# A hybrid layer in one core: two readers of a PSUM bank in a planned order, and the delta rule's state ahead of its output

## The chip, the core and the metric

The kernel runs on one core of a Trainium2 chip. A core has five engines with queues of their own: PE (TensorE, matmuls; PEld is its weight loads), DVE (VectorE, element by element), ACT (ScalarE, functions and copies), POOL (GpSimd) and SP (which issues DMAs here). Each engine takes its instructions in program order and waits on semaphores for the others. PE writes its products into PSUM, eight banks of 512 floats on each of 128 partitions, which ACT and DVE read; everything else lies in SBUF. The metric is the time of one execution on the device in microseconds, lower is better.

## The reference

Two blocks work one after the other on 512 tokens of width 2048. The first projects the tokens, runs a gated delta rule over 24 heads beside an attention over 256 memory rows, and projects back; the second runs an mLSTM and an HGRN2 mixer. The change lies in the delta rule, of which this is the core (chunks `n` of a head, in the kernel 4 chunks of 128 tokens, and the 24 heads in 12 pairs):

```python
def step(state, inp):
    u0_c, w_c, qk_c, qd_c, kd_c, cd_c = inp
    u = u0_c - jnp.einsum("bhcd,bhde->bhce", w_c, state)
    o = jnp.einsum("bhcd,bhde->bhce", qd_c, state) + jnp.einsum("bhcj,bhje->bhce", qk_c, u)
    state = cd_c[..., None, None] * state + jnp.einsum("bhcd,bhce->bhde", kd_c, u)
    return state, o
```

Here `u0` and `w` come from a triangular system of each chunk, solved by an explicit inverse.

## The kernel before

All tensors are float32. A projection multiplies weights and tokens that are each split into a high and a low part, so one step of 128 contracted columns (a k-step below) is three matmuls of 128x512 into one bank named `acc`. Weights arrive in pieces of four k-steps: SP loads `raw`, ACT rounds it to `hi`, DVE subtracts to get `lo`. At most three accumulators are open at once in this stage, and one gives its bank back when its evacuation has read it.

Around the projections run the small tasks. For each pair of heads `inverse` builds the inverse `XT` (`pp`, `px`, two products `p`; on DVE a transpose `Nb` and 31 rounds of a multiply and a reduction on `Xb`), and `rec_task` is the recurrence over the four chunks. One step of it is: `ks` (keys times state, PE), `rp` (two instructions on DVE), `up` (XT times rp, PE, one bank), then two readers of that bank, the copy `u` (ACT), which only the output needs, and the scaled `ud` (DVE), which the next state needs; then `pst` (PE) and the new state `S` (ACT in the first chunk, DVE after), and `o<-e,u` and `o<-gR,S` (PE), the two parts of the output. A recurrence starts only when the one before is done.

What sets the order is a planner that runs when the program is built. `Driver` keeps a clock for each engine, charges every instruction a cost (`act`, `tt`, `stt`, `ts`, `cp` and `mm`), and holds in `tau` when the value at hand will be ready. `run` takes the task of the best priority whose `tau` is not beyond PE's clock, else the next k-step of the projections, else it moves PE's clock on. The program that comes out is fixed: on each engine the instructions stand in that order, and semaphores are the only thing that moves at run time. A semaphore also keeps ACT and DVE from reading one PSUM bank at the same time: the one that is issued second waits for the first.

Two limits of the planner: tiles of 128x512 floats come from 75 slots, and `y_loader`, which fetches for the last gate projections what they multiply, takes a slot only while 24 others stay free, as long as the last recurrence isn't done. And the evacuations of those projections (`evac_z`) wait for that tile, with their accumulators still held.

Of the kernel before, what the change touches and what calls it, by code (L numbers as in the profile page):

```python
# [12 lines left out]
AF = mybir.ActivationFunctionType  # L13
ALU = mybir.AluOpType
AX = mybir.AxisListType
PSUM = bass.MemoryType.PSUM
# [5 lines left out]
NCH = T // C  # L22
# [10 lines left out]
def bc(ap, axis, n):  # L33

    a = ap.unsqueeze(axis)
    return a.broadcast_to(tuple(a.shape[:axis]) + (n,) + tuple(a.shape[axis + 1:]))


def v4(ap):
    return ap.rearrange("p (n c) -> p n c", n=NCH)  # L40


def free_size(ap):
    n = 1
    for s in ap.shape[1:]:
        n *= s
    return n


class Fut:  # L50

    def __init__(self):
        self.done, self.val, self.tau = False, None, 0.0
# [25 lines left out]
class Driver:  # L79
# [5 lines left out]
    def __init__(self, tc, wp, psp, sp):  # L85
        self.tc, self.nc, self.wp, self.psp, self.sp = tc, tc.nc, wp, psp, sp
        self.clk = dict(pe=0.0, act=0.0, dve=0.0, pool=0.0, sp=1.2)
        self.dq = 0.0
        self.tau = 0.0
        self.tasks = []  # L90
        self.units = []
        self.pieces = []
        self.i_unit = self.i_dma = self.i_hi = self.i_spl = self.i_mm = 0
        self.spl_end = []
        self.nbank, self.nacc, self.maxacc = 0, 0, 6
        self.bank_t = [0.0] * 8
        self.bank_of = {}
        self.live = 0
        self._dep, self._last = 0.0, None
        self.held = {}  # L100
        self.nslot = 0
        self.table = None
        self.nhead, self.head = 0, None


    def _on(self, e, cost, lat):
# [2 lines left out]
        self.tau = self.clk[e] + lat  # L109
        self._dep, self._last = dep, (e, self.tau)  # L110

    def act(self, out, in_, func, table=None, **kw):
        t = table or {AF.Exp: 1, AF.Ln: 1, AF.Silu: 2, AF.Sigmoid: 3}.get(func)
        cost = 0.11 + free_size(out) / 1200
        if t and t != self.table:
            self.table = t
            cost += 1.3
            if t == 1:
                self.nc.scalar.add_instruction(mybir.InstLoadActFuncSet(  # L119
                    name=self.nc.get_next_instruction_name(), act_func_set_id=EXP_LN))  # L120
        self.nc.scalar.activation(out=out, in_=in_, func=func, **kw)  # L121
        self._on("act", cost, LV)

    def _v(self, eng, n):
        if eng is None:
            self._on("dve", 0.08 + n / 960, LV)
            return self.nc.vector
        self._on("pool", 0.1 + n / 400, LV)
        return eng

    def tt(self, out, a, b, op, eng=None):
        self._v(eng, free_size(out)).tensor_tensor(out=out, in0=a, in1=b, op=op)  # L132

    def stt(self, out, a, s, b, op0, op1):
        self._v(None, free_size(out)).scalar_tensor_tensor(out=out, in0=a, scalar=s, in1=b, op0=op0, op1=op1)  # L135

    def ts(self, out, a, s1, op0, s2=None, op1=None, eng=None):
        kw = dict(op1=op1) if op1 is not None else {}
        self._v(eng, free_size(out)).tensor_scalar(out=out, in0=a, scalar1=s1, scalar2=s2, op0=op0, **kw)

    def cp(self, out, a, eng=None):
        self._v(eng, free_size(out)).tensor_copy(out=out, in_=a)

    def set(self, out, v, eng=None):
        self._v(eng, free_size(out)).memset(out, v)
# [12 lines left out]
    def mm(self, out, lhsT, rhs, start=True, stop=True, tr=False):  # L158
        n = free_size(out)
        if lhsT.dtype == F32R:  # L160
            c = max(0.107, n / 2400)
        elif tr:
            c = 0.105
        else:
            c = max(0.055 if lhsT.shape[0] <= 32 else 0.107 if lhsT.shape[0] <= 64 else 0.2, n / 600)
            if lhsT.shape[0] <= 64:
                c = min(c, 0.107)
        self.nc.tensor.matmul(out, lhsT=lhsT, rhs=rhs, start=start, stop=stop,  # L168
                              is_transpose=True if tr else None)
        self._on("pe", c, LP)  # L170
# [28 lines left out]
    def free(self, *tiles):  # L199
        self.live -= len(tiles)  # L200
        for t in tiles:
            del self.held[t.tensor.name]

    def small(self, shape, tag, bufs=2):
        return self.sp.tile(list(shape), F32, tag=tag, bufs=bufs, name=tag)

    def bank(self, name="pw"):
        while True:
            if self.nbank >= 8:
                yield lambda: self.nbank < 8  # L210
                continue
            t = self.bank_t[0]
            if max(t, self.tau) <= self.clk["pe"]:
                break
            self.tau = max(t, self.tau)
            yield
        return self.bank_now(name)
# [26 lines left out]
    def give(self, fut, val=True):  # L244
        fut.done, fut.val, fut.tau = True, val, self.tau

    def need(self, fut):
        while not fut.done:
            yield fut
        self.tau = max(self.tau, fut.tau)  # L250
        return fut.val
# [153 lines left out]
def build(ctx: ExitStack, tc: tile.TileContext, A, out):  # L405
# [17 lines left out]
    d = Driver(tc, wp, psp, sp)  # L423
    d.nslot = NSLOT
    act, tt, stt, ts, cp, mm = d.act, d.tt, d.stt, d.ts, d.cp, d.mm
# [33 lines left out]
    n = 0  # L459
# [27 lines left out]
    def split(src, hi, lo):  # L487
        act(hi, src, AF.Copy)
        tt(lo, src, hi, SUB)
# [553 lines left out]
    def rec_task(g):  # L1043
        if g:
            yield from need(f_r[g - 1])
        kT, XT = yield from need(f_k[g])
        qds, e2s, cd, Kt, q2 = yield from need(f_q[g])
        vb0 = yield from need(f_v[2 * g])
        vb1 = yield from need(f_v[2 * g + 1])
        vbs = [vb0, vb1]  # L1050
        o0 = yield from bank("o")
        o1 = yield from bank("o")
        os_ = [o0, o1]
        S = None
        for n in range(NCH):
            s = slice(n * C, (n + 1) * C)
            if n:
                yield
                ks = yield from bank("ks")
                mm(ks[:, :256], kT[:, s], S.rearrange("p h c -> p (h c)"))  # L1060
                t0 = d.tau
                for hh in range(2):
                    mm(os_[hh][:, s], S[:, hh], qds[hh][:, s], start=True, stop=False)
                d.tau = t0
                rp = small([128, 2, C], "rp")
                for hh in range(2):
                    stt(rp[:, hh], ks[:, hh * C:(hh + 1) * C],
                        gate["nbeg"][:, n, 2 * g + hh:2 * g + hh + 1], vbs[hh][:, n], MUL, ADD)
                d.free_bank()
                rr = [rp[:, 0], rp[:, 1]]  # L1070
            else:
                rr = [vbs[0][:, 0], vbs[1][:, 0]]
            yield
            up_ = yield from bank("up")
            up = up_[:, :256].rearrange("p (h c) -> p h c", h=2)
            for hh in range(2):
                mm(up[:, hh], XT[hh][:, n], rr[hh])
            u = small([128, 2, C], "u")
            t0 = d.tau
            act(u, up, AF.Copy)  # L1080
            tu = d.tau
            d.tau = t0
            if n < NCH - 1:
                ud = small([128, 2, C], "ud")
                tt(ud, up, bc(gate["kdec"][:, n, 2 * g:2 * g + 2], 2, C), MUL)
                d.free_bank()
                yield
                ps_ = yield from bank("pst")
                pst = ps_[:, :256].rearrange("p (h c) -> p h c", h=2)
                mm(pst, Kt[:, n], ud.rearrange("p h c -> p (h c)"))  # L1090
                Sn = small([128, 2, C], "S", 3)
                if n:
                    for hh in range(2):
                        stt(Sn[:, hh], S[:, hh], cd[:, hh, n:n + 1], pst[:, hh], MUL, ADD)
                else:
                    act(Sn, pst, AF.Copy)
                d.free_bank()
                S = Sn
                ts_ = d.tau
            else:  # L1100
                d.tau = max(d.tau, tu)
                d.free_bank()
            d.tau = tu
            yield
            for hh in range(2):
                mm(os_[hh][:, s], u[:, hh], e2s[hh][:, n], start=(n == 0), stop=True)
            if n < NCH - 1:
                d.tau = max(ts_, d.clk["pe"])
        free(kT, Kt, *XT, *qds, *e2s, *vbs)
        give(f_r[g])  # L1110
        left = [q2, q2]
        for hh in range(2):
            d.spawn(out_task(2 * g + hh, os_[hh], left), 11 + g)
# [925 lines left out]
```

## Time and profile before

| | |
|---|---|
| three runs | 2903.46, 2903.51 and 2904.26 us, median 2903.51 us |
| the profiled execution | 2903.78 us, of which the span of the trace is 2902.0 us |
| PE busy | 2857.8 us, 98% of the span |
| DVE busy | 1720.4 us, 59% |
| ACT busy | 1409.6 us, 49% |
| the 12 recurrences | from about 408 to 1265 us of the span |

The profile lists for each engine when it was busy, and for the idle time ahead of an instruction which other engine's instruction ended it. PE is the engine to watch: its weight loads overlap its matmuls, and whatever time it stands still is added to the end. A line number in a row is often that of a helper (L121 is every ACT instruction, L132 and L135 most of DVE's, L168 every matmul), so rows are told apart by the names of their tiles, output first. `hi`, `lo` and `acc` belong to the projections. The granted clock is 1.00 when TensorE runs at 2.4 GHz and 0.50 at 1.2 GHz.

### The profile page before, as it was taken

Reading aid. Unit: us, or ns where it says so; the run is one execution under the profiler, and the core shown is the slowest. Engines: PE = TensorE matmul, PEld = TensorE weight load, DVE = VectorE, ACT = ScalarE, POOL = GpSimd, SP = SyncE. Lnnn points to the kernel's source line nnn. Section 1 sums busy time; section 2 is a strip of 40 time slices with the busy share of each in tenths; the row PEclk is TensorE's granted clock in tenths of the full one; section 3 lists DMA queues with packets and bytes.
Section 4 is the critical chain, followed back from the end, with each engine's and each line's share of the span. In section 5 each row is a group of like instructions: output and inputs, shape, how many; then the busy total and the mean of one; then the engine's idle time right before and its main releaser. Section 6 shows DMA issues by size and latency. Waiting matters only on the chain. (4 is left out here: it accounts for less than half of the span.)

```text
span 2902.0 us, 41149 instructions
## 1 busy us (share of the span) xinstructions
PE 2857.8 (98%) x15032; PEld 2392.6 (82%) x15032; DVE 1720.4 (59%) x3287; ACT 1409.6 (49%) x2651; POOL 102.6 (4%) x198
## 2 busy tenths in 40 slices
PE   8999999999999999999999999999999999999998
PEld 7877888788888878888888888888888888888887
DVE  6745677777777767745333364556655655544446
ACT  7544645555555555544222334445555556433444
POOL 2000000000000000000000000000000000000001
PEclk9999999999999999999999999999999999999999
DMA  7423323232322322344433433222222222333224
GB/s 237 149 77 96 123 88 98 95 102 81 102 95 92 98 88 95 106 167 123 127 122 119 139 116 105 93 82 82 83 81 81 88 85 86 117 120 111 93 96 149
DMA packets 179020, 311.05 MB, mean 107 GB/s; under 512 B 25344, under 2 KB 32128, under 8 KB 178816
## 3 DMA queue, kind: packets, MB, share of 16 engines
q1 hardware_dynamic: 178816, 308.41, 33.2%
q8 instruction: 118, 1.93, 0.3%
q14 instruction: 86, 0.70, 0.1%
HBM read 292.34 MB, written 15.99 MB: 106 GB/s over the span
## 5 line engine op out<-in xcount | busy, mean ns | idle before, releaser
L132 DVE TENSOR_TENSOR lo<-raw,hi 128x512 fp32r<-128x512 f32 (+1 forms) x956 | 646.6, 689 | 606.5 <-ACT hi L121 583.0
L121 ACT ACTIVATE hi<-raw 128x512 fp32r<-128x512 f32 (+1 forms) x964 | 591.8, 621 | 846.1 <-PE acc L168 745.2
L168 PE MATMUL acc<-xh,hi 128*128 128x512 f32 x1424 | 583.1, 410 | 0.0
L168 PE MATMUL acc<-xl,hi 128*128 128x512 f32 x1424 | 555.7, 390 | 0.0
L168 PE MATMUL acc<-xh,lo 128*128 128x512 f32 x1408 | 551.1, 391 | 2.4 <-DVE lo L132 2.4
L168 PE MATMUL acc<-x2h,hi 128*128 128x512 f32 x1040 | 415.6, 400 | 0.0
L168 PE MATMUL acc<-x2l,hi 128*128 128x512 f32 x1040 | 405.2, 390 | 0.0
L168 PE MATMUL acc<-x2h,lo 128*128 128x512 f32 x1024 | 399.7, 390 | 0.0
L168 PEld LDWEIGHTS acc<-xh,lo 128*128 128x128 f32 x1408 | 264.4, 188 | 61.6 <-DVE lo L132 3.6
L168 PEld LDWEIGHTS acc<-xh,hi 128*128 128x128 f32 x1424 | 268.2, 188 | 52.2 <-issue 1.7
L168 PEld LDWEIGHTS acc<-xl,hi 128*128 128x128 f32 x1424 | 268.4, 189 | 50.4 <-issue 1.7
L168 PE MATMUL acc<-ph,hi 128*128 128x512 f32 x768 | 298.8, 389 | 0.0
L168 PE MATMUL acc<-pl,hi 128*128 128x512 f32 x768 | 298.8, 389 | 0.0
L168 PE MATMUL acc<-ph,lo 128*128 128x512 f32 x768 | 298.8, 389 | 0.0
L168 PEld LDWEIGHTS acc<-x2h,lo 128*128 128x128 f32 x1024 | 192.2, 188 | 41.4
L168 PEld LDWEIGHTS acc<-x2h,hi 128*128 128x128 f32 x1040 | 195.6, 188 | 37.2
L168 PEld LDWEIGHTS acc<-x2l,hi 128*128 128x128 f32 x1040 | 195.7, 188 | 37.0
L168 PEld LDWEIGHTS acc<-ph,lo 128*128 128x128 f32 x768 | 144.1, 188 | 30.0
L168 PEld LDWEIGHTS acc<-pl,hi 128*128 128x128 f32 x768 | 144.1, 188 | 30.0
L168 PEld LDWEIGHTS acc<-ph,hi 128*128 128x128 f32 x768 | 144.1, 188 | 29.8
L135 DVE SCALAR_TENSOR_TENSOR cv<-acc,c_dn_conv,cv 128x511 f32<-128x511 f32 x144 | 107.2, 747 | 21.3 <-ACT cv L121 17.8
L132 DVE TENSOR_TENSOR Xb<-Xb,Nb 128x16 f32<-128x16 f32 (+30 forms) x372 | 114.5, 308 | 8.7
(323 smaller groups left out, 3712.8 us busy)
## 6 DMA issues: line engine op xcount, KB each, us to landing
raw<-w_qkv SPq DMA_DIRECT2D x192, 256.0 KB, 3.2
raw<-w_out SPq DMA_DIRECT2D x192, 256.0 KB, 2.9
raw<-w_z SPq DMA_DIRECT2D x128, 256.0 KB, 3.1
raw<-w_pg SPq DMA_DIRECT2D x76, 256.0 KB, 3.2
gR<-dgc SPq DMA_DIRECT2D x48, 256.0 KB, 4.1
raw<-w_k SPq DMA_DIRECT2D x32, 256.0 KB, 5.4
raw<-w_v SPq DMA_DIRECT2D x32, 256.0 KB, 3.4
raw<-w_xq SPq DMA_DIRECT2D x32, 256.0 KB, 3.1
```

Source lines behind the costliest of these rows:

```text
L121: self.nc.scalar.activation(out=out, in_=in_, func=func, **kw)
L132: self._v(eng, free_size(out)).tensor_tensor(out=out, in0=a, in1=b, op=op)
L135: self._v(None, free_size(out)).scalar_tensor_tensor(out=out, in0=a, scalar=s, in1=b, op0=op0, op1=op1)
L168: self.nc.tensor.matmul(out, lhsT=lhsT, rhs=rhs, start=start, stop=stop, is_transpose=True if tr else None)
```

## The change

Two things change. In the step of the recurrence `ud` is issued ahead of `u`, so that DVE reads the bank first and ACT second; the planner's time for `u` then lies behind `ud`, and the bank counts as free only after `u`. And the planner notes who last read a PSUM bank: an instruction that reads a bank last read by another engine is timed behind it.

```diff
+def in_psum(ap):
+    return ap.tensor.space == "PSUM"
...
+    def _reads(self, e, *aps):
+        self._bank = [ap.tensor.name for ap in aps if in_psum(ap)]
+        for b in self._bank:
+            if b in self.reader and self.reader[b][0] != e:
+                self.tau = max(self.tau, self.reader[b][1])
+
+    def _read(self, e):
+        for b in self._bank:
+            self.reader[b] = (e, self.tau)
+
     def act(self, out, in_, func, table=None, **kw):
+        self._reads("act", in_)
...
         self._on("act", cost, LV)
+        self._read("act")
...
     def tt(self, out, a, b, op, eng=None):
+        self._reads("dve", a, b)
         self._v(eng, free_size(out)).tensor_tensor(out=out, in0=a, in1=b, op=op)
+        self._read("dve")
...
             u = small([128, 2, C], "u")
-            t0 = d.tau
-            act(u, up, AF.Copy)
-            tu = d.tau
-            d.tau = t0
             if n < NCH - 1:
                 ud = small([128, 2, C], "ud")
                 tt(ud, up, bc(gate["kdec"][:, n, 2 * g:2 * g + 2], 2, C), MUL)
-                d.free_bank()
+            td = d.tau
+            act(u, up, AF.Copy)
+            tu = d.tau
+            d.free_bank()
+            d.tau = td
+            if n < NCH - 1:
                 yield
...
                 ts_ = d.tau
-            else:
-                d.tau = max(d.tau, tu)
-                d.free_bank()
             d.tau = tu
```

`stt`, `ts` and `cp` get the same two lines as `tt`. No instruction is added; two ACT table loads fall away. The order is the same in both programs up to the first recurrence, and again from within the last gate projections on; between them it differs on every engine. With `in_psum` answering no, the new program comes out the same row for row, so the order below is due to the new place of `u` and `ud` alone, and the reading in turn moves nothing in it.

Counted in k-steps of the projections that stand ahead of its first matmul on PE, the 12 recurrences start at 613, 700, 794, 879, 981, 1073, 1163, 1238, 1316, 1403, 1481 and 1559 before, and at 613, 702, 790, 881, 983, 1077, 1172, 1271, 1364, 1463, 1536 and 1573 now.

The first place is PE in the eleventh recurrence. Before, its first step runs so (`e_10634` and `e_10673` are the two heads' parts of `e`):

```order
L168 MATMUL acc<-xh,lo 128x512
L168 MATMUL pst<-ud,Kt 128x256
L168 MATMUL o<-e_10634,u 128x128
L168 MATMUL o<-e_10673,u 128x128
L168 MATMUL acc<-xh,hi 128x512
L168 MATMUL acc<-xl,hi 128x512
L168 MATMUL acc<-xh,lo 128x512
L168 MATMUL ks<-S,cv 128x256
L168 MATMUL o<-gR,S 128x128 x2
L168 MATMUL acc<-xh,hi 128x512
```

And now, on PE in the same recurrence, from the end of the inverse:

```order
L194 MATMUL acc<-xh,lo 128x512
L194 MATMUL p_12192<-XT,gR 64x64 x8
L194 MATMUL p_12213<-P_12088,XA 64x64 x8
L194 MATMUL up<-vb,XT 128x128 x2
L194 MATMUL pst<-ud,Kt 128x256
L194 MATMUL o<-e_10672,u 128x128
L194 MATMUL o<-e_10701,u 128x128
L194 MATMUL ks<-S,cv 128x256
L194 MATMUL o<-gR,S 128x128 x2
L194 MATMUL up<-rp,XT 128x128 x2
```

The k-steps that stood between its matmuls are gone: from the first product `p` to the last `o<-e,u` of the fourth step no `acc` stands on PE any more, while before 32 k-steps stood in nine of the ten gaps from the first `up` on (4, 1, 1, 3, 1, none, 9, 7, 4 and 2), and other tasks' products in the tenth.

The second place is DVE in the same recurrence, from the first `ud` on. Before:

```order
L132 TENSOR_TENSOR ud<-up,kdec 128x256
L132 TENSOR_TENSOR lo<-raw,hi 128x512
L132 TENSOR_TENSOR Xb<-Xb,Nb 128x8x8
L909 TENSOR_REDUCE Xb<-Xb 128x8
L132 TENSOR_TENSOR Xb<-Xb,Nb 128x8x9
L909 TENSOR_REDUCE Xb<-Xb 128x8
L132 TENSOR_TENSOR Xb<-Xb,Nb 128x8x10
L909 TENSOR_REDUCE Xb<-Xb 128x8
L135 SCALAR_TENSOR_TENSOR rp<-ks,nbeg,vb 128x128 x2
```

And now, on DVE (`Xb` and `Nb` are the twelfth pair's inverse):

```order
L151 TENSOR_TENSOR ud<-up,kdec 128x256
L151 TENSOR_TENSOR Xb<-Xb,Nb 128x8x5
L935 TENSOR_REDUCE Xb<-Xb 128x8
L151 TENSOR_TENSOR Xb<-Xb,Nb 128x8x6
L935 TENSOR_REDUCE Xb<-Xb 128x8
L151 TENSOR_TENSOR Xb<-Xb,Nb 128x8x7
L935 TENSOR_REDUCE Xb<-Xb 128x8
L156 SCALAR_TENSOR_TENSOR rp<-ks,nbeg,vb 128x128 x2
L151 TENSOR_TENSOR Xb<-Xb,Nb 128x8x8
L935 TENSOR_REDUCE Xb<-Xb 128x8
```

Three rounds of `Xb` stand in each gap between `ud`, `S` and `rp` now, seven gaps from the first `ud` to the third `rp`; the `lo` of the projections, and other tasks' work in the later gaps, stand there no more.

The third place is ACT ahead of the copy `u` in the first step of the ninth recurrence. Before:

```order
L121 ACTIVATE XT<-p_10386 64x4x64 x2
L121 ACT_TABLE_LOAD
L121 ACTIVATE cv<-cv 128x512 x4
L121 ACTIVATE sz<-sz 128x512 x2
L121 ACTIVATE hi<-raw 128x512
L121 ACTIVATE u<-up 128x256
```

And now, on ACT:

```order
L138 ACTIVATE XT<-p_10645 64x4x64 x2
L138 ACTIVATE cv<-acc,c_dn_conv 128x512
L138 ACTIVATE hi<-raw 128x512
L138 ACTIVATE u<-up 128x256
L138 ACTIVATE hi<-raw 128x512 x2
```

The table load and the six functions behind it no longer stand ahead of this `u`, and `ud` on DVE no longer waits for any `u`.

## Rows read from the trace of the kernel before

**Rows 1.** The page: busy time of each engine, share of the span, instructions

```profile
PE 2857.8 (98%) x15032; PEld 2392.6 (82%) x15032; DVE 1720.4 (59%) x3287; ACT 1409.6 (49%) x2651; POOL 102.6 (4%) x198
```

**Rows 2.** Busy time by stretch, PE to POOL: recurrences' stage; eleventh recurrence; a quiet stretch

```profile
400.00:1300.00 900.00, 890.74 (x5389) 739.26 (x5388) 666.04 (x1504) 483.50 (x1027) 57.27 (x129) 1.00 0.31 101
1176.50:1210.50 34.00, 34.00 (x182) 29.24 (x183) 28.24 (x78) 14.63 (x27) 1.51 (x3) 1.00 0.30 95
1400.00:1500.00 100.00, 100.00 (x442) 82.80 (x442) 32.10 (x47) 26.54 (x42) 0.00 (x0) 1.00 0.40 123
```

**Rows 3.** PE's waits within 400 to 1300 us: total, times, longest

```profile
PE pst L168 <- DVE ud L132: 3.8, 2, 3.1
PE acc L168 <- DVE lo L132: 2.4, 3, 1.5
PE px L168 <- ACT P L121: 1.4, 1, 1.4
```

**Rows 4.** Ninth recurrence, first step, in order of time: start, length, instruction, idle before

```profile
1023.15 1.28 ACT L121 ACT_TABLE_LOAD   x1
...
1026.54 1.13 ACT L121 ACTIVATE sz<-sz 128x512 f32<-128x512 f32 x2
...
1028.10 0.36 ACT L121 ACTIVATE u<-up 128x256 f32<-128x256 f32 x1
1028.49 0.42 DVE L132 TENSOR_TENSOR ud<-up,kdec 128x256 f32<-128x256 f32 x1 [4.87 <-ACT u L121]
1028.97 1.22 PE L168 MATMUL pst<-ud,Kt 128*128 128x256 f32 x2 [3.11 <-DVE ud L132]
```

**Rows 5.** The stretch in which the granted clock (PEclk) was halved

```profile
1027.97:1034.80 6.83, 5.83 (x22) 5.37 (x23) 4.61 (x12) 2.02 (x5) 0.25 (x1) 0.50 0.05 20
```

**Rows 6.** DVE's waits within 400 to 1300 us: ud behind u

```profile
DVE ud L132 <- ACT u L121: 15.0, 10, 4.9
```

**Rows 7.** Twelfth recurrence, first step, PE in order of time

```profile
1246.26 0.60 PE L168 MATMUL up<-vb,XT 128*128 128x128 f32 x4
...
1248.08 0.59 PE L168 MATMUL pst<-ud,Kt 128*128 128x256 f32 x2
1248.51 0.61 PE L168 MATMUL o<-e,u 128*128 128x128 f32 x4
1248.87 0.48 PE L168 MATMUL acc<-xh,hi 128*128 128x512 f32 x1
...
1249.65 0.60 PE L168 MATMUL ks<-S,cv 128*128 128x256 f32 x2
1250.09 0.61 PE L168 MATMUL o<-gR,S 128*128 128x128 f32 x4
```

**Rows 8.** The same on ACT, with the copies ahead of the step

```profile
1242.27 0.59 ACT L121 ACTIVATE P<-p 64x512 f32<-64x512 f32 x1 [2.26 <-PE p L168]
...
1244.88 0.65 ACT L121 ACTIVATE XT<-p 64x256 f32<-64x256 f32 x2 [1.37 <-PE p L168]
1246.90 0.38 ACT L121 ACTIVATE u<-up 128x256 f32<-128x256 f32 x1 [1.38 <-PE up L168]
```

**Rows 9.** Eleventh recurrence, DVE in order of time

```profile
1187.41 0.60 DVE L135 SCALAR_TENSOR_TENSOR S<-S,cd,pst 128x128 f32<-128x128 f32 x2 [0.69 <-PE pst L168]
1187.93 0.27 DVE L132 TENSOR_TENSOR Xb<-Xb,Nb 128x112 f32<-128x112 f32 x1
...
1189.70 0.60 DVE L135 SCALAR_TENSOR_TENSOR rp<-ks,nbeg,vb 128x128 f32<-128x128 f32 x2
...
1193.33 0.29 DVE L132 TENSOR_TENSOR Xb<-Xb,Nb 128x136 f32<-128x136 f32 x1
...
1195.25 0.68 DVE L132 TENSOR_TENSOR vb<-tr,beta 128x512 f32<-128x512 f32 x1
...
1196.44 0.42 DVE L132 TENSOR_TENSOR ud<-up,kdec 128x256 f32<-128x256 f32 x1
1196.78 0.69 DVE L132 TENSOR_TENSOR sq<-sq,sz 128x512 f32<-128x512 f32 x1
```

More of the change, by code (lines that the diff above doesn't have):

```diff
@@ L102, in __init__ @@
         self.table = None
+        self.reader, self._bank = {}, []
         self.nhead, self.head = 0, None
@@ L131, in tt @@
     def tt(self, out, a, b, op, eng=None):
+        self._reads("dve", a, b)
         self._v(eng, free_size(out)).tensor_tensor(out=out, in0=a, in1=b, op=op)
+        self._read("dve")
     def stt(self, out, a, s, b, op0, op1):
+        self._reads("dve", a, b)
         self._v(None, free_size(out)).scalar_tensor_tensor(out=out, in0=a, scalar=s, in1=b, op0=op0, op1=op1)
+        self._read("dve")
     def ts(self, out, a, s1, op0, s2=None, op1=None, eng=None):
+        self._reads("dve", a)
         kw = dict(op1=op1) if op1 is not None else {}
         self._v(eng, free_size(out)).tensor_scalar(out=out, in0=a, scalar1=s1, scalar2=s2, op0=op0, **kw)
+        self._read("dve")
     def cp(self, out, a, eng=None):
+        self._reads("dve", a)
         self._v(eng, free_size(out)).tensor_copy(out=out, in_=a)
+        self._read("dve")
     def set(self, out, v, eng=None):
```

## The prediction, made before the changed kernel had run

> **What bounds the kernel now.** I read the page first: PE is busy for 2857.8 of 2902.0 us, DVE for 59% [rows 1]. What PE still idles can be won, and each idle microsecond added to PE comes out at the end. Then I cut the span, because the order differs only around the recurrences: there PE is busy for 890.74 of 900 us, so 9.26 us of idle time can be won at most, and in the quiet stretch it is full, with 442 matmuls in 100 us [rows 2]. So a k-step of three matmuls takes 0.68 us. PE's waits say what ended those idle times: 3.8 us were waits of `pst` for `ud`, in two places, 3.1 us of it at one; the rest are waits for `lo` and for the pieces of the inverse [rows 3]. That one place is in the ninth recurrence: on ACT a table load, functions and a `hi` ran ahead of the copy `u`, which came only at 1028.10; `ud`, second reader of the bank, began at 1028.49 after 4.87 us of idle DVE, and PE stood still for 3.11 us [rows 4]. Behind it the granted clock was halved to 1.2 GHz for 6.83 us, with PE busy for 5.83 of them [rows 5]: 5.83 / 2 = 2.9 us of matmul time lost. So the stage holds 9.26 + 2.9 = 12.2 us that a better order could give back.
>
> Weight loads alone would tell another story: they fill 739.26 of the 900 us, 82% [rows 2]. The Trainium skill (Perfetto Trace Analysis, Identifying the Most-Contended Engine) calls matmul busy time a bad measure and wants weight-load busy time instead; by that 18% of the stage would be free and an idle gap might cost nothing. The quiet stretch shows 82.80 with PE at 100.00 [rows 2], so 82% is what a full PE shows in this kernel, and the trace decides against that reading.
>
> **The change, part by part.** *The reading in turn* costs and brings nothing by itself: without it the order is the same.
>
> *`ud` ahead of `u`.* DVE waited for `u` before `ud` ten times, 15.0 us in all [rows 6]. That wait is gone in all 36 steps; of it PE felt 3.8 us, and I take the halved clock with it: gain 3.8 + 2.9 = 6.7 us. In exchange `u` waits for `ud`, 0.42 us [rows 4], and behind `u` on ACT are queued `hi` pieces of the projections, for whose `lo` PE waits. ACT is busy for 483.5 of 900 us [rows 2] and pieces are made up to five ahead, so I cost this at nothing; if that cover fails it shows as waits of `acc` for `lo`, 2.4 us now [rows 3].
>
> *The order that comes out of it.* The recurrences drift back against the projections, by 33 to 60 k-steps from the eighth to the eleventh. The other 9.26 - 3.8 = 5.5 us of idle time have causes that the change doesn't touch (`lo` behind other work on DVE, the inverse's small products); they get dealt anew. I take them as unchanged, with 0 and 11 us as bounds.
>
> *The eleventh recurrence stands bare.* Before, this recurrence ran at about 1178 to 1209 us with PE busy for 34.00 of 34.00 us [rows 2], since 32 k-steps, some 22 us of work, filled its gaps. Now nothing fills them. The reason is in the planner's limits: the accumulators of the gate projections wait for tiles that `y_loader` can't get before this recurrence frees its own. The total of PE's work is the same, so what PE idles in the bare stretch is lost. Its length follows from the chain, link by link:
>
> - From product `p` to `up`: ACT's copy `P` 0.59 us and copy `XT` 0.65 us [rows 8], each with about 0.1 us for the handoffs at both ends (`up` ends at 1246.86 and `u` starts at 1246.90; `ud` ends at 1028.91 and `pst` starts at 1028.97) [rows 4, 7, 8]. PE idles for both: 1.5 us. `up` takes 0.60 us from its start to its end but holds PE for 0.36 only, as four matmuls of `o` do (1248.51 to 1248.87) [rows 7]: 0.3 us with the handoff. Sum 1.8 us.
> - First step, from the start of `ud` to `rp`: `ud` 0.42, handoff 0.06, `pst` 0.59, handoff 0.04, the copy `S` on ACT as long as `u`, 0.38, handoff 0.06, `ks` 0.60, handoff 0.04: 2.19 us [rows 4, 7, 8].
> - From there to the end of the third `rp`, DVE is the limit, since three rounds of `Xb` stand in each of six gaps. Three rounds took 1.77 us at widths 112 to 128 (1187.93 to 1189.70) and 1.92 us at 136 to 152 (1193.33 to 1195.25) [rows 9]; these are the middle two of the six (widths 64 to 200), so six gaps take 6 x 1.845 = 11.1 us. Between them stand two `rp` and two `S` at 0.52 (1187.41 to 1187.93), two `ud` at 0.34 (1196.44 to 1196.78) and the last `rp` at 0.60 [rows 9]: 3.4 us. Sum 14.5 us. What PE and ACT have to do in a gap (handoff, `up`, handoff: 0.7 us; `pst` or `ks` the same) is shorter than three rounds and costs nothing there.
> - From the third `rp` to the last `o`: 0.06 + 0.60 + 0.04 + 0.38 + 0.06 = 1.14 us.
>
> From the first `ud` to the last `o` that is 2.19 + 14.5 + 1.14 = 17.8 us. In them PE holds three times `pst` 0.43 (1248.08 to 1248.51), `ks` 0.44, and `o<-e,u`, `o<-gR,S` and `up` at 0.36 each [rows 7]: 3 x 1.95 = 5.85 us. Idle: 11.9 us, and with the 1.8 us ahead 13.7 us.
>
> *Behind it.* After four k-steps the sum of squares needs a value that stands behind six more rounds on DVE; and the clock may be low when PE resumes. Either costs some 2 to 3 us and they overlap, since slow k-steps cover the wait. The nearest row is the halved clock after the 3.11 us stall: 2.9 us [rows 5]. I take 2.9 us, with 0 and 6 as bounds.
>
> Inside the stretch a low clock matters less. PE's bursts there are short, with idle time between. The Trainium skill (TensorE: Matmul & The Clock Gate, HAM oscillation) says that matmuls in short bursts between waits keep falling back to half the clock; by that `up`, `pst` and `ks` would double wherever no `Xb` covers them, 4 x 0.6 = 2.4 us more, and the loss would be 19.0 us. No row here shows a recurrence at the low clock; the rows give `pst` 1.22 us at 0.50 [rows 4, 5] against 0.59 at 1.00 [rows 7]. I leave the 2.4 us to the upper end.
>
> *The sum.* Lost: 13.7 + 2.9 = 16.6 us. Won: 6.7 us. Net 9.9 us on 2903.78 us, the profiled execution, is 2913.7 us; the median of the three runs is 0.3 us under that execution, so **2913.4 us**, slower by 0.34%.
>
> **The rivals.** *Everything else is won (about the same).* The bare stretch costs 13.7 us, nothing comes behind it, and all 12.2 us of the stage's old losses vanish: +1.5 us, 2905 us. For it speaks that half of the old stalls are short, so that a small shift of the order removes them; against it that the change removes only the waits for `u`.
>
> *The bare stretch is short (faster).* If DVE had its rounds of `Xb` done before the step that they stand ahead of, only the links would count: a step of `up` 0.64, `ud` 0.48, `pst` 0.63, `S` 0.6, `ks` 0.7 and `rp` 0.66 us is 3.7 us, less 1.95 us of PE's work, 1.8 us idle; three steps and the 1.8 us ahead are 7.2 us. With all 12.2 us won that is 2898.5 us. It decides where the bare stretch costs under 6.7 us. Against it: DVE takes its rows in order, and the rounds stand behind a `ud` that itself waits for `up`, so they can't run early.
>
> *The order is worse throughout (slower still).* The clock stays low in and behind the bare stretch (2.4 us more inside, 6 instead of 2.9 us behind), and the redealt waits double: +5.5 us. Together 11.0 us more, 2924 us. For it: where the recurrences lag, long work of other tasks stands ahead of `lo` on DVE, which is the fuller of the two (666 of 900 us) [rows 2].
>
> That the change doesn't do what it says holds for its first half; the order shows that the second half acts.
>
> **How the numbers follow.** The forecast, with net +6 to +15 us: 0.63. The worse order: 0.20. Everything else won: 0.14. The short bare stretch: 0.03. From the lower bounds of the terms, 13.7 - 12.2 = +1.5 us, 2905 us; from the upper, +21 us, 2924 us; that range leaves out less than 2 in 10, and as the term of the stretch is a sum of many links I put its ends at 2904.5 and 2924. A measurement of this kernel tells about 0.2%, 5.8 us, from no change: faster 0.02, same 0.15, slower 0.83.
>
> **What would show it.** In the profile after: a stretch near 1190 to 1225 us in which PE is busy for only about a third of some 18 us, with waits of `pst`, `ks` and `up` for DVE's `ud`, `S` and `rp`; the granted clock at 0.50 in or right behind it; no wait of `ud` for `u`; PE's idle time of the stage at about 20 us instead of 9.26; the stretches before 400 us and after 1300 us as long as they were. It would be wrong if the recurrence took the time of its bare links, some 11 us, or if the stage's other waits came to well over 11 us.

## The result, and the profile after

The changed kernel takes 2921.43 us (median of four runs, 2919.81 to 2923.03) against 2903.49 us of the kernel before on the same chip: 1.0062 of its time, 95% interval 1.0050 to 1.0074, so 17.9 us slower. The forecast was 2913.4 us with a range to 2924: the sign and the place were right, the size was too small. The 17.9 us lie past the band of +6 to +15 us that the forecast itself had been given, and nearer to the rival of the worse order (2924 us). The profiled execution took 2923.03 us with a span of 2921.2 us.

The busy time by stretch, of the kernel after (columns as in [rows 2]: PE, PEld, DVE, ACT, POOL, then the granted clock, DMA share, GB/s): the stage, the bare stretch, and what comes right behind it.

```profile
400.00:1300.00 900.00, 882.63 (x5318) 729.74 (x5317) 654.67 (x1491) 467.87 (x1008) 56.74 (x129) 0.99 0.30 95
...
1214.32:1242.29 27.97, 17.56 (x88) 14.42 (x89) 22.27 (x75) 5.79 (x17) 2.53 (x7) 0.70 0.28 97
1242.29:1246.17 3.88, 3.88 (x11) 3.11 (x11) 3.03 (x7) 1.67 (x3) 0.00 (x0) 0.50 0.00 0
```

PE's idle time of the stage went from 9.26 us [rows 2] to 17.37 us, and the clock is at half inside the bare stretch and behind it. The 27.97 us hold some 8.8 us of matmul work at the full clock: two products `p` at 1.1 us, and by the lengths that the prediction took from [rows 7] 3 x 1.95 us for the steps and 2 x 0.36 us for the first `up` and the last `o`. So the bare stretch lost 19.2 us. PE's waits of the stage, of the kernel after (total, times, longest), to be held against [rows 3]:

```profile
PE pst L194 <- DVE ud L151: 3.4, 3, 1.6
PE acc L194 <- DVE lo L151: 2.8, 4, 1.3
PE p L194 <- ACT XT L138: 2.4, 1, 2.4
PE ks L194 <- DVE S L156: 1.7, 2, 1.1
```

All three waits of `pst` in the first row lie in the bare stretch; the two of [rows 3] are gone. The stretch itself, PE in order of time (start, length, instruction, idle time before it and what ended it):

```profile
1216.68 1.11 PE L194 MATMUL p<-XT,gR 64*64 64x64 f32 x16 [2.36 <-ACT XT L138]
1218.58 1.71 PE L194 MATMUL p<-P,XA 64*64 64x64 f32 x16 [0.79 <-issue]
1220.75 1.22 PE L194 MATMUL up<-vb,XT 128*128 128x128 f32 x4 [0.47 <-DVE Xb L935]
1222.49 1.22 PE L194 MATMUL pst<-ud,Kt 128*128 128x256 f32 x2 [0.52 <-DVE ud L151]
...
1234.60 1.22 PE L194 MATMUL pst<-ud,Kt 128*128 128x256 f32 x2 [1.58 <-DVE ud L151]
...
1239.66 1.22 PE L194 MATMUL up<-rp,XT 128*128 128x128 f32 x4 [0.35 <-DVE rp L156]
1241.42 1.22 PE L194 MATMUL o<-e,u 128*128 128x128 f32 x4 [0.53 <-ACT u L138]
1242.29 0.77 PE L194 MATMUL acc<-xh,hi 128*128 128x512 f32 x1
```

No k-step stands between 1214.32 and 1242.29 us. `up` takes 1.22 us in the first step and the last, `pst` in the first and the third, twice the 0.60 and 0.59 us of [rows 7]. DVE in the same stretch, in order of time:

```profile
1222.02 0.42 DVE L151 TENSOR_TENSOR ud<-up,kdec 128x256 f32<-128x256 f32 x1 [0.42 <-PE up L194]
...
1225.46 0.61 DVE L156 SCALAR_TENSOR_TENSOR rp<-ks,nbeg,vb 128x128 f32<-128x128 f32 x2 [1.70 <-PE ks L194]
...
1231.69 0.60 DVE L156 SCALAR_TENSOR_TENSOR rp<-ks,nbeg,vb 128x128 f32<-128x128 f32 x2
...
1239.27 0.60 DVE L156 SCALAR_TENSOR_TENSOR rp<-ks,nbeg,vb 128x128 f32<-128x128 f32 x2
```

From the first `rp` on no row of DVE shows a wait: three rounds of `Xb` stand in each gap, and PE waits for DVE.

**How kernels are compared below.** The profiles show that the start, from the first matmul to the first `up` of the first recurrence, takes anything from 399.2 to 404.0 us, although no kernel here changes it. From that `up` to the end of the last matmul a kernel repeats itself: 2482.1 and 2482.6 us in the two profiles of before, 2498.3 and 2498.9 us in the two of after. So beside the ratio of the times this **rest** is given; of the 17.9 us, 16.3 are in it (2498.6 against 2482.3, the means). The profiled execution of after also had the longest start, 404.0 us, against 401.6 and 400.6 us of before.

### The profile page after: what moved, and what is told of

Same layout as the page of the kernel before. It is cut to its first block, busy times and chain, and to the rows that moved or that the text cites. A ratio compares the mean times of both kernels' runs of the same rounds, so it can differ in the third digit from the quotient of the medians.

```text
span 2921.2 us, 41162 instructions
## 1 busy us (share of the span) xinstructions
PE 2867.2 (98%) x15032; PEld 2398.1 (82%) x15032; DVE 1717.9 (59%) x3287; ACT 1404.6 (48%) x2649; POOL 102.9 (4%) x198
## 5 line engine op out<-in xcount | busy, mean ns | idle before, releaser
L935 DVE TENSOR_REDUCE Xb<-Xb 128x8 f32<-128x16 f32 (+30 forms) x372 | 110.4, 297 | 12.8
```

The lines of the kernel that those rows point to most:

```text
L935: nc.vector.tensor_reduce(out=Xb[:, :, i], in_=pr[:, :, 0:i + 1], op=ADD, axis=AX.X)
```

## The experiments

**Theory:** the loss is the bare eleventh recurrence, so it comes from the order, and the swap itself brings something. **Rival A:** the swap itself costs, as `u` waits for `ud` and `hi` pieces stand behind `u` on ACT. **Rival B:** the new order is worse throughout. **Rival C:** the missing k-steps are only moved. Each run is compared with the kernel before on the same chip.

### The swap without its order

The order of before on every engine; only on the chip `ud` reads the bank first. The planner's clocks are set as if `u` had come first:

```diff
             t0 = d.tau
-            act(u, up, AF.Copy)
-            tu = d.tau
-            d.tau = t0
             if n < NCH - 1:
                 ud = small([128, 2, C], "ud")
                 tt(ud, up, bc(gate["kdec"][:, n, 2 * g:2 * g + 2], 2, C), MUL)
+                k0 = (d.tau, d._dep, d._last)
+                d.tau = t0
+            act(u, up, AF.Copy)
+            tu = d.tau
+            d.tau = t0
+            if n < NCH - 1:
+                d.tau, d._dep, d._last = k0
                 d.free_bank()
```

> The kernel before, with its order kept instruction for instruction on every engine; only on the chip `ud` is issued ahead of `u`, so that DVE reads the bank first. It does the change's second half without the order that comes out of it. Theory (the loss is the bare eleventh recurrence, so it comes from the order; the swap by itself brings what the waits of `ud` cost): 3.8 us of PE's waits go, and the halved clock behind the longest of them, 2.9 us, so 2896.8 us against 2903.5, ratio 0.9977; 2899.7 if the clock falls elsewhere instead. Rival A (the swap itself costs, since `u` now waits for `ud` and the `hi` pieces stand behind `u` on ACT): slower than before, up to the change's whole 17.9 us, 2921 us, with waits of `acc` for `lo` and `hi` well over 2.4 us.

Measured: 2900.95 us against 2904.49, ratio 0.9988 (0.9979 to 0.9997). Rest 2481.0 us against 2482.1. The swap doesn't cost, so rival A falls in this order; but it brings less than the 6.7 us. Between the first `up` of the ninth recurrence and that of the tenth the time went from 82.88 to 76.79 us, 6.1 us less, as expected: the wait of 3.11 us and the halved clock behind it [rows 4, 5] are gone. Two things came in their place. Between the second and the third recurrence it went from 83.63 to 87.20 us, since the clock was at half there (by stretch, of this kernel):

```profile
564.16:570.98 6.82, 6.82 (x32) 4.89 (x31) 5.30 (x19) 1.22 (x2) 0.00 (x0) 0.50 0.72 230
```

And from the seventh to the eighth it went from 67.81 to 69.12 us. Three views of this kernel, ACT, DVE and PE in order of time, show why:

```profile
910.90 0.38 ACT L121 ACTIVATE u<-up 128x256 f32<-128x256 f32 x1 [3.48 <-DVE ud L132]
911.18 0.62 ACT L121 ACTIVATE hi<-raw 128x512 fp32r<-128x512 f32 x1
```

```profile
911.84 0.69 DVE L132 TENSOR_TENSOR lo<-raw,hi 128x512 fp32r<-128x512 f32 x1 [1.03 <-ACT hi L121]
...
914.82 0.59 DVE L135 SCALAR_TENSOR_TENSOR S<-S,cd,pst 128x128 f32<-128x128 f32 x2
```

```profile
915.56 0.67 PE L168 MATMUL ks<-S,cv 128*128 128x256 f32 x2 [0.76 <-DVE S L135]
```

`u` waits for `ud`, a `hi` stands behind `u`, DVE waits 1.03 us for that `hi` ahead of `lo`, and the rounds of `Xb` and `S` behind it are late, so that PE waits 0.76 us for `S` where before it had no wait: rival A's chain, at one place, in a stretch that grew by 1.3 us.

> The kernel of e1_old_order_ud_first once more on this chip: the swap in the order of before. Theory: faster than before by 2 to 7 us, ratio 0.9975 to 0.9993, as the 3.8 us of waits are gone and the halved clock behind them may or may not fall elsewhere. Rival A (the swap by itself brings nothing or costs): 0.9995 or more.

On another chip: 2901.14 us against 2904.67, ratio 0.9987 (0.9978 to 0.9995), rest 2481.5 us, and the halved spell again, at 565 us. A second profile of the kernel before:

> The kernel before once more, for a second profile of it. The profile of before has one halved spell of the clock in the stage, at 1028 us, and none at 564 us; both profiles with `ud` first in the same order (e1, e11) have it at 564 us instead, behind a wait of 1.4 us that before has too. If the spell at 564 us is the swap's, this profile has only that at 1028 us again; if it is chance, it may have one at 564 us too. In either case the 3.1 us wait of `pst` for `ud` in the ninth recurrence comes back within 0.1 us, and the start, up to the first recurrence's `up`, differs from the first profile's 401.6 us by 0 to 3 us.

It has the halved spell at 1027 us alone and the wait of 3.11 us again; 2903.50 us, start 400.6 us. So the spell at 564 us goes with the swap in all four profiles. Whether it stands in the executions without a profile is not shown: the profiled ones took 2903.32 and 2904.65 us, 2.4 and 3.5 us above the medians of their runs, and the medians gained 3.5 us on before where the rest gained 1.0. PE stands still for 1.4 us just ahead of it in both kernels; why the clock falls there in one of them alone stays open.

### The order without the swap

The changed kernel's order on every engine, with `u` first on the chip (the planner still counts `ud` first):

```diff
             if n < NCH - 1:
                 ud = small([128, 2, C], "ud")
+                nc.scalar.activation(out=u, in_=up, func=AF.Copy)
                 tt(ud, up, bc(gate["kdec"][:, n, 2 * g:2 * g + 2], 2, C), MUL)
-            td = d.tau
-            act(u, up, AF.Copy)
+                td = d.tau
+                d._reads("act", up)
+                d._on("act", 0.11 + 2 * C / 1200, LV)
+                d._read("act")
+            else:
+                td = d.tau
+                act(u, up, AF.Copy)
             tu = d.tau
```

> The changed kernel, with its order kept instruction for instruction on every engine; only on the chip `u` is issued ahead of `ud` again. It has the order that comes out of the change without the swap. Theory (order): the whole loss stays, 2921.4 us, and waits of `ud` for `u` come back wherever ACT is late, 0 to 4 us of them felt by PE: 2921 to 2925 us, ratio 1.006 to 1.0075. Rival A (the swap itself costs): near the kernel before, 2903.5 us.

Measured: 2920.26 us, ratio 1.0052 (1.0040 to 1.0065), rest 2500.9 us. The whole loss is there without the swap: **the order is the cause**. DVE waited 12.2 us for `u` ahead of `ud` in this run:

```profile
DVE ud L151 <- ACT u L1107: 12.2, 10, 5.1
```

but outside the bare stretch no wait of `pst` for `ud` reached PE (three waits, 3.6 us, all inside it). So in this order the 3.8 us of [rows 3] are gone whichever of the two reads first; it was not the swap that won them.

### The changed kernel without the bare stretch

```diff
-            t = yield from slot(name="y", reserve=lambda: 4 if f_r[NH - 1].done else 24)
+            t = yield from slot(name="y", reserve=lambda: 4 if f_r[NH - 1].done else 8)
```

> The changed kernel with the reserve of `y_loader` at 8 tiles instead of 24: its tiles come before the eleventh recurrence starts, the accumulators of the gate projections have work, and by the order some 37 k-steps stand between the eleventh recurrence's products and 20 between the twelfth's. All before the eleventh recurrence keeps the changed kernel's order. Theory (bare stretch): of the 25.6 us from `p` of the eleventh recurrence to the next k-step some 17 us of PE's idle time go, and the slow clock in and behind it, 4 to 5 us: 2899 to 2905 us, ratio 0.9985 to 1.0005. Rival B (the order is worse throughout, the recurrences lag everywhere): the gain is under half of the loss, 2913 us or more. Rival C (the missing k-steps are only moved, and PE idles as long in the twelfth or behind it): 2916 us or more.

Measured: 2903.47 us against 2904.49, ratio 0.9995 (0.9986 to 1.0004), rest 2481.4 us against the changed kernel's 2498.6. One number in one line takes back all of the loss. PE has no idle time in the eleventh and the twelfth recurrence (first `up` at 1224.15 and 1284.82 us), so rival C falls. By stretch, of this kernel:

```profile
1213.50:1300.00 86.50, 86.50 (x559) 72.05 (x551) 53.88 (x134) 39.49 (x78) 2.61 (x7) 1.00 0.39 133
```

The order is that of the changed kernel up to some 1190 us, late in the tenth recurrence, where the first of `y_loader`'s tiles come earlier; so rival B falls too. What is left is ahead of the eleventh, one wait of PE, and the clock is at half for 3.4 us behind it:

```profile
1209.80 0.54 PE L194 MATMUL acc<-xh,lo 128*128 128x512 f32 x1 [3.02 <-DVE lo L151]
```

What no run separates is why the new place of `u` and `ud` lets the recurrences drift back so far: `u` timed behind `ud`, or the bank freed only after `u`.

### The reading in turn alone

The kernel before with the change's first half, `u` still ahead of `ud` (the diff is that of the change without its last two pieces).

> The kernel before with the change's first half alone: the order's model lets engines that share a bank read it in turn, and `u` stays ahead of `ud`. By the order the recurrences then start at the k-steps 613, 700, 793, 884, 972, 1060, 1145, 1216, 1309, 1395, 1483 and 1556, close to the kernel before, none of them bare. Theory (bare stretch): no loss; the short stalls are dealt anew, and as the model now knows that `ud` waits for `u`, fewer products are placed too early: 2898 to 2906 us, ratio 0.998 to 1.001. Rival B (any redealt order of this stage is worse, since the old one was fitted by hand to the model's old times): 2910 us or more.

Measured: 2899.03 us, ratio 0.9978 (0.9969 to 0.9987); rest 2478.8 us. It is **faster than both kernels**: 7.4 us of PE's idle time in the stage instead of 9.26, and the halved spell takes 3.4 us instead of 6.8. Both came again on another chip:

> The kernel of e4_in_turn_only once more, beside that of e7_in_turn_ud_first, since those two ran on different chips and at different halved-clock spells (3.4 us against 6.8 in the stage). Theory G (the order of e4 is better than that of before by its shorter stalls: 7.4 us of PE's idle time in the stage instead of 9.3): faster than before again, ratio 0.997 to 0.9995. Rival H (its 5.5 us were chance, of the clock): 0.9995 to 1.001.

2900.29 us, ratio 0.9982 (0.9973 to 0.9991), rest 2479.1 us, so theory G holds. Of the some 3.3 us of the rest 1.7 to 1.8 are idle time and 1.7 the shorter spell, which was so in both profiles. The stage by stretch, of this run:

```profile
400.00:1300.00 900.00, 892.41 (x5402) 740.98 (x5401) 667.71 (x1505) 480.93 (x1026) 59.71 (x129) 1.00 0.32 101
```

Now both halves of the change with this order kept: `ud` first on the chip, while the planner counts `u` first:

```diff
             t0 = d.tau
+            if n < NCH - 1:
+                ud = small([128, 2, C], "ud")
+                nc.vector.tensor_tensor(out=ud, in0=up, op=MUL,
+                                        in1=bc(gate["kdec"][:, n, 2 * g:2 * g + 2], 2, C))
             act(u, up, AF.Copy)
             tu = d.tau
             d.tau = t0
             if n < NCH - 1:
-                ud = small([128, 2, C], "ud")
-                tt(ud, up, bc(gate["kdec"][:, n, 2 * g:2 * g + 2], 2, C), MUL)
+                d._reads("dve", up)
+                d._on("dve", 0.08 + 2 * C / 960, LV)
+                d._read("dve")
                 d.free_bank()
```

> The kernel with the reading in turn alone (run e4_in_turn_only), its order kept instruction for instruction on every engine; only on the chip `ud` is issued ahead of `u`. Both halves of the change act, but the order doesn't follow the second. Theory: e4_in_turn_only had no wait of `pst` for `ud` of over 20 ns left to win, so the swap brings nothing more: within 2 us of its 2899.0, ratio to the kernel before 0.997 to 0.9985. Rival A' (the swap is worth 3.5 us in any order, as in e1_old_order_ud_first): 2895.5 us, ratio 0.9966.

Measured: 2902.28 us, ratio 0.9998 (0.9989 to 1.0007), rest 2482.1 us: no gain, and 3.3 us more of the rest. Since the two had run on different chips, they ran once more side by side:

> The kernel of e7_in_turn_ud_first once more, beside that of e4_in_turn_only. If `u` behind `ud` costs something where no `ud` waited for `u`, it is slower than e9_in_turn_only_again by 1.5 us or more, as the stage of e7 was (855.99 us against 852.69). If the difference was the clock's, the two agree within 1 us.

2902.54 us against the 2900.29 of the run beside it, rest 2480.8 against 2479.1 us, with halved spells of 3.4 us in both. So where no `ud` held PE up, the swap costs some 2 us, in the two profiles of this pair at five recurrences by 0.2 to 0.6 us each. PE's shown idle time is the same in both (7.6 us); the steps that grow are those ahead of `ks` and `ks` itself. That this is the chain of `hi` and `lo` behind `u` again is likely, but not shown.

### What sets the length of the bare stretch

The changed kernel once more, to compare the next two with:

> The changed kernel once more, beside the three runs that change it, so that differences of a few us can be read. All theories expect 2919 to 2923 us; where its own runs spread by 3 us, differences under 1.5 us are not told apart.

2919.91 us, ratio 1.0057 (1.0044 to 1.0070), rest 2498.9 us. First the rounds of `Xb` taken out of the stretch:

```diff
         if g:
             yield from need(f_rows[g - 1])
+        if g == NH - 1:
+            yield from need(f_r[g - 1])
         Xp = yield from slot((128, 2, 8, 32), name="Xb")
```

> The changed kernel with the last inverse held back until the eleventh recurrence is done. By the order the eleventh recurrence stays bare (no k-step from its first `up` to its last `o`), but no round of `Xb` stands on DVE between its steps; the twelfth then starts at k-step 1616 instead of 1573. Theory (DVE's rounds of `Xb` set the length of the bare stretch, 14.5 of its 17.8 us as predicted): only the links are left, 2.19 + 0.6 + 2 x 3.7 + 1.14 = 11.4 us from the first `ud` to the last `o` at the full clock, up to 16.2 us if eight products run at half of it, against 19.4 us in the changed kernel; 3 to 8 us less, 2913 to 2918 us. Rival D (the links and the slow clock set it, the rounds of `Xb` fit into the time that they leave): within 1.5 us of the changed kernel, 2919.5 to 2922 us, with 18 us or more from the first `ud` to the last `o`.

Measured: 2914.47 us, ratio 1.0035 (1.0023 to 1.0048), rest 2491.0 us, 7.9 us less than the changed kernel. PE in order of time, of this kernel:

```profile
1210.92 1.14 PE L194 MATMUL p<-XT,gR 64*64 64x64 f32 x16
...
1215.70 0.88 PE L194 MATMUL pst<-ud,Kt 128*128 128x256 f32 x2 [0.52 <-DVE ud L151]
...
1228.16 0.71 PE L194 MATMUL o<-e,u 128*128 128x128 f32 x4 [0.53 <-ACT u L138]
1228.63 0.48 PE L194 MATMUL acc<-xh,hi 128*128 128x512 f32 x1
...
1231.81 0.50 PE L194 MATMUL ss<-qh,ones_r 128*128 128x512 f32 x1 [2.23 <-ACT qh L138]
```

From the first `ud` (1215.22 us) to the last `o` it takes 12.94 us instead of 19.40, within the 11.4 to 16.2 us of the links alone: DVE's rounds did set the length, and rival D falls. The wait of 2.36 us ahead of `p` is gone as well. Of the 10 to 11 us that the stretch is shorter by (against the two profiles of the changed kernel), about 2.5 come back behind it as waits of `ss`, which in the changed kernel has none there.

Then the rounds left in, and PE kept busy in its waits:

```diff
+    def fill(g, n, out, w, x):
+        for _ in range(n if g == NH - 2 else 0):
+            nc.tensor.matmul(out[:, :256], lhsT=w, rhs=x, start=True, stop=True)
...
+        fill(g, 4, p2_, Mn[0][:, 0], Mn[0].rearrange("p n c -> p (n c)")[:, :256])
...
+                fill(g, 2, ks, Kt[:, n], kT[:, :256])
...
+            fill(g, 1, up_, Kt[:, n], kT[:, :256])
...
+                fill(g, 2 if n else 1, ps_, Kt[:, n], kT[:, :256])
```

(and one ahead of the inverse's last product).

> The changed kernel with 20 matmuls more in and just ahead of the eleventh recurrence: each writes a PSUM tile that the products behind it overwrite, so they only keep PE busy in its waits (4 and 1 ahead of the inverse's last two products, 1 or 2 ahead of each `up`, `pst` and `ks`). Nothing else of the order changes. Theory (the slow clock is a cost of its own, about 2.4 us inside the stretch, 2.0 behind it and some in its first link): the granted clock stays at 1.00, `pst`, `ks` and `up` take 0.6 us instead of 1.2, and the time is 3 to 5 us less than that of the changed kernel, 2916 to 2918.5 us. Rival E (DVE sets the length, so that a product at half speed costs nothing, and the k-steps behind are slow for 2 us only): 0 to 2 us less, 2919.5 to 2921.5 us. Rival F (the added matmuls stand in the way of the products): slower than the changed kernel by up to 20 x 0.2 = 4 us.

Measured: 2921.01 us, ratio 1.0059 (1.0046 to 1.0071), rest 2498.5 us: the changed kernel's time, rival E. From the first `pst` on the clock did stay up; only the products just ahead of it ran at half (by stretch, then PE in order of time, of this kernel):

```profile
1216.47:1219.89 3.42, 3.42 (x17) 2.74 (x15) 2.65 (x11) 0.79 (x3) 0.00 (x0) 0.50 0.78 239
1219.89:1243.78 23.89, 18.13 (x93) 13.48 (x92) 20.39 (x68) 3.48 (x8) 0.00 (x0) 1.00 0.12 43
```

```profile
1231.42 0.70 PE L194 MATMUL pst<-ud,Kt 128*128 128x256 f32 x2 [0.90 <-DVE ud L151]
...
1238.23 0.47 PE L194 MATMUL acc<-xh,hi 128*128 128x512 f32 x1
...
1243.02 0.49 PE L194 MATMUL ss<-qh,ones_r 128*128 128x512 f32 x1 [1.78 <-ACT qh L138]
```

From the last k-step ahead of the stretch to the next one it took 26.7 us (1211.57 to 1238.23) against 29.1 us (1210.56 to 1239.61) in the run beside it: 2.4 us won. But the k-steps behind then ran at full speed into the sum of squares, which waited 1.78 us, and 0.23 us more for its second part, and behind that wait the clock was at half for another 3.4 us. So what the fuller clock won inside was given back at once behind the stretch, as far as 5 executions of each kernel tell.

## Why the prediction was right, and where it was too small

**Right: the cause.** The order, not the swap, makes the loss (second experiment), and it makes it where the prediction said, since tiles for `y_loader` come too late (third experiment). DVE's three rounds in each gap set the length: from the first `rp` to the end of the third it took 14.4 us (1225.46 to 1239.87), predicted 14.5. Behind it the slow clock covered the wait of `ss`, as predicted: `ss` has no wait there in the kernel after, and of the predicted 2.9 us 1.9 came (3.88 us at half the clock). In the run with PE kept busy the wait came instead, but the slow clock came behind it as well, so it is not one *or* the other.

**Too small: the bare stretch, 13.7 predicted, 19.2 measured.** Two things make up the 5.5 us.

*The chain began too late in the working, 2.4 us.* I started it at the product `p`. But `p` itself waited 2.36 us (the first of PE's rows of the stretch, above), and that wait has the same cause as the rest: the last inverse begins there, and its copies stand on ACT ahead of the `XT` that `p` needs, themselves waiting for DVE. ACT in order of time, of the kernel after:

```profile
1214.34 0.31 ACT L138 ACTIVATE Xb<-gR 32x128 f32<-32x128 f32 x1 [1.53 <-DVE gR L156]
1214.99 0.82 ACT L138 ACTIVATE Xb<-gR 32x128 f32<-32x128 f32 x3 [0.35 <-DVE gR L156]
1215.83 0.42 ACT L138 ACTIVATE Xb<-c_xinit 128x256 f32<-128x256 f32 x1
1216.27 0.43 ACT L138 ACTIVATE XT<-px 32x128 f32<-32x128 f32 x2
```

With that inverse held back the wait was gone.

*The clock inside the stretch, 3.2 us.* The prediction put it at nothing in its sum and left it to a rival, for want of a row of a recurrence at the low clock. It is the sum of four links: from `p` to the first `ud` 5.34 us instead of 4.3 (two `p` at 1.1 us, 1.5 us for the copies, 0.6 for `up`), from there to the first `rp` 3.44 instead of 2.19, from the third `rp` to the last `o` 1.55 instead of 1.14, and 0.87 us from that `o` to the next k-step instead of 0.36. Where DVE sets the pace, slow products cost nothing: 14.4 us came where 14.5 were predicted. In the second profile of the changed kernel both products `p` ran at half the clock (1.94 us each) and the stretch took 29.05 us, 1.1 more. The Trainium skill (TensorE: Matmul & The Clock Gate, HAM oscillation) describes this falling back in short bursts between waits; the trace agrees in kind, with a mean granted clock of 0.70 in the stretch, and by that rule the prediction had worked out 2.4 us, of the 3.2 that came. The run with PE kept busy says that as a saving it is worth nothing here, as the wait of `ss` and the slow clock behind it take its place.

**The other waits, 5.5 predicted, 7.0 measured.** 4.9 us at 462 to 558 us, and 2.0 us just ahead of the bare stretch, at 1203 to 1210 us. Well within the bounds of 0 and 11.

**The gain, 6.7 predicted.** Both parts are gone from the profile after, so the term is right in size. Its reason is not: with `u` first in the new order they are gone too, and in the old order the swap took 6.1 us away and gave back nearly 5 of it, by a halved spell elsewhere (with a short wait of `ks`, 3.6 us) and by late `hi` (1.3 us): the rest is 1.1 us shorter. So in the old order the 2.9 us of the clock were not won: another spell came. What I costed at nothing, `hi` behind `u`, costs 1.3 us at the one place where it is shown, and perhaps the some 2 us of the swap beside the reading in turn.

**The sum.** 19.2 + 1.9 + 1.5 - 6.7 = 15.9 us, against 16.3 us of the rest. The remaining 1.6 of the 17.9 us lie in the start, which differs from run to run; in the second run of the changed kernel the difference to before was 16.8 us.

**The signs.** The waits of `pst`, `ks` and `up` for DVE and the halved clock came as named. That PE would be busy for only a third of the stretch did not: between the first `ud` and the last `o` it was busy for 12.65 of 19.40 us, since a product counts as busy from its start to its end, 0.6 us where the sum let it hold PE for 0.36 to 0.44 [rows 7], and up to 1.22 us at half the clock. So PE's idle time of the stage (17.37 us, predicted about 20) shows only a part of the loss.

**A sentence that was too wide.** The reading in turn "costs and brings nothing by itself" holds only beside the swap. Without the swap it changes the order too, to one that is 4 to 5 us faster than before.

**The rivals.** That everything else would be won (2905 us) fell, since the stretch cost more and the other waits grew. The short bare stretch (2898.5 us) fell as well: the bare links alone, 12.94 us from the first `ud` to the last `o`, came only when the rounds were taken out. The rival of the worse order had the slow clock inside the stretch right; its other two terms, 6 us behind the stretch and doubled waits, did not come. That 2921 us lies within the range is owed to the range's upper end, where this rival stands, and not to the sum.

## What to carry to other kernels

Look in the order for a stretch where the bounding engine has nothing to put between the links of a dependent chain, and find which reserve or limit keeps its filler away; here one number, 24 instead of 8, was worth 17 us, over twice the 6.7 us of stalls that the change could remove. Start the sum of such a stretch at the last full-speed instruction ahead of it, not at the chain's first link, because the copies that feed the first link stand in the same queues as what delays the later ones. A removed stall is worth what the next wait leaves of it, so ask what the work behind was hidden by, and compare profiles by stages that repeat themselves rather than by whole times.

## What the runs showed of the hardware

The stage and all behind it repeat within 0.6 us of some 2490 in four of the five kernels that were profiled twice, three of the five on two chips (1.2 us in the fifth, where a halved spell was 3.4 us longer), while the start of the same instructions varies by nearly 5 us; a difference of 2 us between profiles is more than that spread if the start is left out. With the swap in the old order one halved-clock spell went and another came: none at 1028 us any more, but one at 564 us, behind a stall of 1.4 us that had been there before with the clock at 1.00; what decides this is open. And two engines that read one PSUM tile do take turns: in the first experiment `ud` ends at 910.81 and `u` starts at 910.90 us after 3.48 us of idle ACT. The Trainium skill (PSUM — Partial Sum Buffer, PSUM bank collisions raise a hardware error) says that the compiler's scheduler orders any two instructions on different engines that touch the same 32 partitions of one bank, reads too; the wait that the change turned round is of this kind.
